# Moving the elementwise work off POOL in a two-layer hybrid attention and mixture-of-experts encoder

## The chip, the cores and the metric

The kernel runs on 1 core of a Trainium2 chip. The metric is device microseconds of one execution; the median of three runs of the kernel before is 1399.47 us (1397.34 to 1400.84). The engines are named as in the profile: PE (matmul), PEld (its weight loads), DVE (vector), ACT (scalar), POOL (GpSimd), SP (sync, which here only issues DMAs).

## The reference

Two layers over x of 512 tokens by 1024 channels, all in float32, with a conditioning vector c. Each layer does:

```
mod = silu(c) @ w_ada[l] + b_ada[l];  sh1, sc1, g1, sh2, sc2, g2 = split(mod, 6)
h   = layer_norm(x) * (1 + sc1) + sh1
mix = mixer(h)
x   = layer_norm(ALPHA * x + g1 * mix, ln1_g, ln1_b)
h   = layer_norm(x) * (1 + sc2) + sh2
ffn = moe(h)
x   = layer_norm(ALPHA * x + g2 * ffn, ln2_g, ln2_b)
```

The mixer projects h once (w_in), runs a global grouped-query attention (branch A, 8 heads) and a dilated windowed attention (branch B, three groups of 4 heads, joined by their softmax denominators), then computes (g_a * (out_a @ w_pa) + g_b * (out_b @ w_pb)) @ w_o with sigmoid gates. The mixture of experts scores 16 experts, picks the best group of four and the two best experts in it, and adds their SwiGLU outputs (256 hidden channels each) with normalised weights.

## The kernel before

The 512 tokens are 4 tiles of 128 (`NT`). A product that must hold float32 accuracy is split: each operand is rounded to a high part (ACT, `ACT.copy` to float32r), the low part is the difference (DVE, `tensor_sub`), and three matmuls are summed (`gemm3`, L220). Weights are split the same way in `wsplit` (L195; cast L215, subtraction L216, 520 of each at 128x512). The order of instructions on each engine follows the program's order and the framework's own ordering by readiness; `tc.issue_after` (an instruction isn't issued before another) adjusts it in ten places. Every engine works through its queue in order, and a DMA is issued by the engine whose queue it is written on: SP (`SY`), ACT or POOL (`PO`).

The stages of a layer, with the names and lines that the change touches:

- **Head.** `head_first` (L349, layer 0) norms x, transposes it, applies scale and shift per channel (`apply`, L374) and makes the high part (ACT, L377) and the low part (L378), the odd k on POOL. `head_next` (L390) does the same for layer 1, tile by tile; the low part (L413) of group j = 3 (`HLP`) is on POOL.
- **Projections, attention.** `first_q`, `fill_b`, `fill_g`, `rope`, branch A and branch B. POOL takes a power for the RMS norm (`pool_rsqrt`, L283), zeroes two key tiles per layer, and in layer 0 writes zeros to the expert output y2 by DMA.
- **Join and merge.** `join` (L886) weights branch B's three groups and adds them: the first addition on POOL (L892), the second on DVE (L893). The merge loop (L908 to L919) multiplies branch B's product by its gate (L915), adds branch A (L916; odd c, `PBPO`, on POOL), and splits the sum (ACT L918, DVE L919).
- **Output projection, norms.** For tile t and block b of 256 columns `out_block` (L941) multiplies the product by g1 (DVE, L947) and adds it to the residual xr (L948, POOL but for the two blocks in `XDVE`). `tile_x1` transposes xr for the router (PE), takes statistics and norms xr to x1; `tile_h2` norms x1 to h2, which a DMA on SP's queue stores to `h2d` in DRAM (L978). `norm` (L313): the first `cut` columns on DVE in two `scalar_tensor_tensor` steps (L321, L323), the rest on ACT (L319, scale and bias) and POOL (L325 times g, L326 plus b). `cut` is 768 for x1 and for xo, 896 for h2, 1024 for x1 of tile 3.
- **Router.** The last h2 is finished behind the sigmoid: ACT scales it (L1006), POOL adds the shift (L1007), in halves, and SP stores it (L1008). Expert weights ahead of use are loaded on SP's queue from L997 on. DVE compares scores in the tile `versus`, cleared by POOL (L1026), and with PE builds the index tile `vt` (L1076). POOL clears three tiles `xe` (L1100), then gathers the rows of expert e from `h2d` by an indirect DMA (`x_load`, L1106).
- **Expert loop.** For 16 experts: `x_split`, `x_gate`, `x_up` (the product with SiLU, L1138), `x_down` (products L1175, scaled by g2 L1176, scattered to y2 by an indirect DMA on POOL, L1180; the last two experts' outputs are kept in SBUF).
- **Combine.** y2 comes back in 8 tiles on SP's queue (L1296). `rows_in` adds them to x1 with their weights: `scalar_tensor_tensor` on DVE (L1306), except (t, 0) of every tile t (`PROWS`), where ACT scales (L1303) and POOL adds (L1304). The rows of tile 0 are added ahead of `x_down` of the last expert, those of tile 1 behind its first mark, those of tiles 2 and 3 behind its third (`SPLIT`). `combine` (L1332) adds the kept experts and x1 on PE in PSUM (L1312, L1335); `finish` (L1339) norms to xo and stores it, and in layer 0 goes on to layer 1's head.

`stats` (L300) issues on DVE the statistics (L303, L305) and var + eps (L285), then on POOL the power (L286) and minus mean times it (`nb`, L308).

Of the kernel before, what the change touches and what calls it, by code (L numbers as in the profile page):

```python
# [8 lines left out]
F32 = mybir.dt.float32  # L9
# [3 lines left out]
AF = mybir.ActivationFunctionType  # L13
# [12 lines left out]
NG = 4  # L26
# [61 lines left out]
def build(tc, A, out):  # L88
    nc = tc.nc
    with ExitStack() as es:  # L90
# [222 lines left out]
        def norm(src, name, g, b, st=None, cut=None):  # L313

            cut = cut or CUT
            m, r, nb = st or stats(src)
            n = f4(name, [D])
            for p, z in parts(src, cut, D) if cut < D else []:
                issued["act"] = ACT.activation(n[:, z], p, AF.Identity, bias=nb, scale=r)  # L319
            for p, z in parts(src, 0, cut):  # L320
                V.scalar_tensor_tensor(n[:, z], p, m, g[:, z], op0=OP.subtract, op1=OP.mult)  # L321
            a, z = slice(0, cut), slice(cut, D)
            issued["dve"] = V.scalar_tensor_tensor(n[:, a], n[:, a], r, b[:, a], op0=OP.mult, op1=OP.add)  # L323
            if cut < D:
                PO.tensor_tensor(n[:, z], n[:, z], g[:, z], op=OP.mult)  # L325
                PO.tensor_tensor(n[:, z], n[:, z], b[:, z], op=OP.add)  # L326
            return n
# [21 lines left out]
        def head_first(xt):  # L349
# [24 lines left out]
            def apply(k):  # L374
                z, H, L = (u[k // 2][:, k % 2, :] for u in (zT, hH, hL))
                i = V.tensor_scalar(z, z, mcol[0, 1][:, k:k + 1], mcol[0, 0][:, k:k + 1], op0=OP.mult, op1=OP.add)
                ACT.copy(H, z)  # L377
                (PO if k % 2 else V).tensor_tensor(L, z, H.bitcast(F32), op=OP.subtract)  # L378
                return i
# [10 lines left out]
        def head_next(l):  # L390
# [4 lines left out]
            def tile_in(t, x, st):  # L395
# [3 lines left out]
                for q in range(2):  # L399
# [10 lines left out]
                    for j in range(2 * q, 2 * q + 2):  # L410
                        f, H, L = F[:, 2 * j:2 * j + 2, :], hH[j][:, :, tcols(t)], hL[j][:, :, tcols(t)]
                        ACT.copy(H, f)  # L412
                        i = (PO if j in HLP else V).tensor_tensor(L, f, H.bitcast(F32), op=OP.subtract)  # L413
                        if j not in HLP:
                            issued["head"] = i
# [14 lines left out]
        def layer(l, hH, hL, W0, after=None, qk=None):  # L430
# [455 lines left out]
            def join():  # L886
                for i in range(2):
# [4 lines left out]
                    PO.tensor_tensor(oB[0][:, i, :], oB[0][:, i, :], oB[1][:, i, :], op=OP.add)  # L892
# [15 lines left out]
            for b in range(2):  # L908
                WB = wsplit(wb[:, 512 * b:512 * b + 512].rearrange("(k p) n -> p k n", p=P), [2, 512])
                for c in range(4):  # L910
# [5 lines left out]
                    (PO if c in PBPO else V).tensor_tensor(ga, ga, gb, op=OP.add)  # L916
# [22 lines left out]
            x1, r1, LAST = [], [], []  # L939

            def out_block(t, b):  # L941
# [6 lines left out]
                (V if (t, b) in XDVE else PO).tensor_tensor(xr[t][:, cb], xr[t][:, cb], y, op=OP.add)  # L948

            def tile_x1(t):  # L950
# [9 lines left out]
                n = norm(xr[t], "x1", r_g, r_b, st, D if t == NT - 1 else None)  # L960
# [4 lines left out]
            def tile_h2(t):  # L965
                n = x1[t]
                st = stats(n)
                V.scalar_tensor_tensor(sco[:, t], lg[:, t], r1[t], brow, op0=OP.mult, op1=OP.add)
                V.scalar_tensor_tensor(sco[:, t], sco[:, t], st[1], rrow, op0=OP.mult, op1=OP.add)
                if t < NT - 1:  # L970
                    n2 = norm(n, "h2", r_sc2, r_sh2, st, CUTH)
                    ACT.mul(n, n, ALPHA)
                else:
                    n2 = f4("h2", [D])
                    V.scalar_tensor_tensor(n2, n, st[0], r_sc2, op0=OP.subtract, op1=OP.mult)
                    LAST.append((n2, st[1]))
                    return
                SY.dma_start(h2d[tcols(t), :], n2)  # L978
# [21 lines left out]

            sig = ACT.activation(sco, sco, AF.Sigmoid)
            with tc.issue_after(sig.ins):
                n2, r = LAST[0]
                for i in range(2):
                    z = slice(512 * i, 512 * i + 512)
                    ACT.mul(n2[:, z], n2[:, z], r)  # L1006
                    PO.tensor_tensor(n2[:, z], n2[:, z], r_sh2[:, z], op=OP.add)  # L1007
                SY.dma_start(h2d[tcols(NT - 1), :], n2)  # L1008
                ACT.mul(x1[NT - 1], x1[NT - 1], ALPHA)
            sel = rt("sel", [NT, NE])  # L1010
# [14 lines left out]
            versus = sc("versus", [(NT + 1) * NG, 16])  # L1025
            PO.memset(versus, 0.0)  # L1026
# [70 lines left out]

            xes = [f4("xe", [D]) for _ in range(NXE)]
            for z in xes:
                PO.memset(z, 0.0)  # L1100
# [198 lines left out]
            def rows_in(n):  # L1299
                for _ in range(2 * n):  # L1300
                    t, k, y = ys.pop(0)
                    if (t, k) in PROWS[l]:
                        ACT.mul(y, y, gt[:, k, t:t + 1])  # L1303
                        PO.tensor_tensor(x1[t], x1[t], y, op=OP.add)  # L1304
                    else:
                        V.scalar_tensor_tensor(x1[t], y, gt[:, k, t:t + 1], x1[t], op0=OP.mult, op1=OP.add)  # L1306
# [32 lines left out]
            def finish(t):  # L1339
                y, st = Y.pop(t)  # L1340
                n = norm(y, "xo", r_g, r_b, st, CUT2[l])
# [22 lines left out]
HLP = (3,)  # L1364
XDVE = ((3, 2), (3, 3))
# [8 lines left out]
PROWS = (((0, 0), (1, 0), (2, 0), (3, 0)),) * 2  # L1374
EKEEP = 2
CUTH = 896
PBPO = (1, 3)
# [7 lines left out]
CUT = 768  # L1385
NPE = 3
CUT2 = (768, 768)
# [25 lines left out]
```

## Time and profile before

| | before |
|---|---|
| median of 3 runs | 1399.47 us |
| the profiled execution's own time | 1398.57 us |
| its span, first to last instruction | 1396.8 us |
| PE busy | 1278.9 us (92%) |
| PEld busy | 1039.7 us (74%) |
| DVE busy | 1024.2 us (73%) |
| ACT busy | 720.2 us (52%) |
| POOL busy | 282.4 us (20%) |
| mean granted PE clock | 0.967 of full speed |
| DMA | 266.76 MB, mean 191 GB/s |

Times in the profile are microseconds from the span's start unless marked ns. A row of a timeline is a start, a duration, the engine, the line of the kernel, the operation, output <- inputs, the count and, in brackets, how long the engine stood idle before it and what ended that. Queues of the engines that only issue carry a q (ACTq, SPq).

### The profile page before, as it was taken

What the parts mean: (1) busy time and instruction counts of PE and PEld (TensorE: products, weight loads), DVE (VectorE), ACT (ScalarE), POOL (GpSimd) and SP (SyncE); (2) the same over time, 40 slices, a digit from 0 to 9 for tenths busy, and PEclk for the clock granted to TensorE, in tenths of its full rate; (3) what the DMA queues carried; (4) which work ended last, traced back from release to release, by engine and by line L of the source; (5) the groups of instructions that cost most, each with busy time, mean ns of one, the idle gap of its engine ahead of it and who ended that gap; (6) DMA issues with size and microseconds to landing.
All of it is one profiled execution on the core that took longest, in us unless ns stands there. A gap on an engine that the chain in (4) does not pass through costs nothing. (4 is left out here: it accounts for less than half of the span.)

```text
span 1396.8 us, 21644 instructions
## 1 busy us (share of the span) xinstructions
PE 1278.9 (92%) x7953; PEld 1039.7 (74%) x7953; DVE 1024.2 (73%) x1974; ACT 720.2 (52%) x1506; POOL 282.4 (20%) x273
## 2 busy tenths in 40 slices
PE   5898999999998949999889999999999894999986
PEld 4797777677777938888659787767777784888862
DVE  5877777767367778999798877564336767899985
ACT  2344444555644237777645444455565522777760
POOL 1132000000002651221341300000000256222224
PEclk9999999999999969999999999999999996999998
DMA  9646654556155187999653555122214536799952
GB/s 317 218 156 239 208 167 167 154 185 218 32 174 204 61 272 260 308 346 338 233 182 125 160 181 170 61 76 76 76 46 151 180 122 218 272 301 344 352 206 84
DMA packets 182992, 266.76 MB, mean 191 GB/s; under 512 B 18665, under 2 KB 131721, under 8 KB 182880
## 3 DMA queue, kind: packets, MB, share of 16 engines
q1 hardware_dynamic: 159312, 225.46, 48.4%
q0 software_dynamic: 11456, 24.07, 4.9%
q10 hardware_dynamic: 12112, 15.78, 3.7%
q8 instruction: 64, 1.05, 0.3%
q14 instruction: 48, 0.39, 0.1%
HBM read 250.79 MB, written 27.30 MB: 199 GB/s over the span
## 5 line engine op out<-in xcount | busy, mean ns | idle before, releaser
L216 DVE TENSOR_TENSOR wL<-raw,wH 128x512 fp32r<-128x512 f32 x520 | 349.9, 703 | 67.3 <-ACT wH L215 52.0
L215 ACT CAST wH<-raw 128x512 fp32r<-128x512 f32 x520 | 318.9, 622 | 148.4 <-PE mm L1175 41.6
L225 PE MATMUL mm<-hH,wH 128*128 128x512 f32 x512 | 206.4, 403 | 0.0
L226 PE MATMUL mm<-hL,wH 128*128 128x512 f32 x512 | 202.4, 395 | 0.0
L227 PE MATMUL mm<-hH,wL 128*128 128x512 f32 x512 | 202.0, 394 | 0.0
L225 PE MATMUL mm<-wH,xH 128*128 128x256 f32 x512 | 149.1, 291 | 1.0 <-ACT xH L343 1.0
L227 PE MATMUL mm<-wH,xL 128*128 128x256 f32 x512 | 148.9, 291 | 0.9 <-DVE xL L344 0.9
L226 PE MATMUL mm<-wL,xH 128*128 128x256 f32 x512 | 146.6, 286 | 0.3 <-DVE wL L216 0.3
L249 DVE SCALAR_TENSOR_TENSOR acc<-araw,cond,acc 128x512 f32<-128x512 f32 x148 | 110.7, 749 | 5.5 <-DMA araw<-in_w_ada 2.3
L227 PEld LDWEIGHTS mm<-hH,wL 128*128 128x128 f32 x512 | 96.2, 188 | 21.1 <-issue 1.1
L225 PEld LDWEIGHTS mm<-hH,wH 128*128 128x128 f32 x512 | 96.3, 188 | 20.1 <-issue 1.2
L226 PEld LDWEIGHTS mm<-hL,wH 128*128 128x128 f32 x512 | 96.3, 188 | 19.1 <-issue 0.3
L225 PEld LDWEIGHTS mm<-wH,xH 128*128 128x128 f32 x512 | 99.0, 193 | 3.1 <-ACT xH L343 2.0
L226 PEld LDWEIGHTS mm<-wL,xH 128*128 128x128 f32 x512 | 98.9, 193 | 2.4 <-DVE wL L216 1.2
L227 PEld LDWEIGHTS mm<-wH,xL 128*128 128x128 f32 x512 | 98.6, 192 | 2.3 <-DVE xL L344 1.8
L225 PE MATMUL mm<-wH,hH 128*128 128x256 f32 (+1 forms) x272 | 81.7, 301 | 4.6 <-ACT hH L412 2.8
L227 PE MATMUL mm<-wH,hL 128*128 128x256 f32 (+1 forms) x272 | 81.2, 300 | 2.1 <-DVE hL L378 0.7
L226 PE MATMUL mm<-wL,hH 128*128 128x256 f32 (+1 forms) x272 | 80.5, 296 | 0.1
L1180 POOL DMA_INDIRECT y<-ye,vt x28 | 33.6, 1202 | 209.8 <-DVE ye L1176 209.8
L281 POOL DMA_DIRECT2D mod<-adar x8 | 4.3, 532 | 331.4 <-ACT adar L280 331.4
L1175 PE MATMUL mm<-raw,eT 128*128 128x512 f32 x128 | 65.4, 635 | 3.6 <-ACT eT L1158 1.5
L745 DVE TENSOR_TENSOR zB<-sB,biasB 128x256 f32<-128x256 f32 (+2 forms) x48 | 22.8, 488 | 61.4 <-PE sB L743 27.7
(316 smaller groups left out, 2873.0 us busy)
## 6 DMA issues: line engine op xcount, KB each, us to landing
araw<-in_w_ada SPq DMA_DIRECT2D x44, 1024.0 KB, 5.3
raw<-in_w_in SPq DMA_DIRECT2D x40, 1024.0 KB, 5.2
raw<-in_w_exp_gate SPq DMA_DIRECT2D x32, 1024.0 KB, 9.3
raw<-in_w_exp_up SPq DMA_DIRECT2D x28, 1024.0 KB, 12.4
raw<-in_w_exp_down SPq DMA_DIRECT2D x28, 1024.0 KB, 10.0
raw<-in_w_out SPq DMA_DIRECT2D x8, 1024.0 KB, 7.2
y<-y SPq DMA_DIRECT2D x16, 512.0 KB, 8.4
eraw<-in_w_ada SPq DMA_DIRECT2D x4, 1024.0 KB, 16.0
```

The source lines that it names most:

```text
L215: ACT.copy(H, raw(s))
L216: V.tensor_sub(L, raw(s), H.bitcast(F32))
L225: PE.matmul(o, lhsT=lH, rhs=rH, start=(i == 0), stop=False)
L226: PE.matmul(o, lhsT=lH, rhs=rL, start=False, stop=False)
L227: PE.matmul(o, lhsT=lL, rhs=rH, start=False, stop=(i == n - 1))
L249: last = V.scalar_tensor_tensor(acc, raw[:, k, :], ck, acc, op0=OP.mult, op1=OP.add)
L281: PO.dma_start(moddr[l, kind].rearrange("o (k n) -> (o k) n", n=P), r[0:8, :])
L745: V.tensor_add(z, s[:, :, 0:wid], biasB[g][:, ii::2, j0:j0 + wid])
L1175: PE.matmul(p, lhsT=a, rhs=w, start=(i == 0), stop=(i == len(todo) - 1))
L1180: st = PO.indirect_dma_start(out=y2, out_offset=bass.IndirectOffsetOnAxis(ap=vidx[:, e:e + 1], axis=0), in_=ye, in_offset=None, bounds_che ...
```

## The change

All elementwise instructions of POOL but the small ones of `stats` and of the RMS norm, and the zeroing of key tiles, go to DVE; the clearing of `versus` and of the xe tiles goes to ACT, which multiplies a row by zero. `norm` no longer divides a tile between engines: two steps on DVE for columns 0 to 255 and 256 to 1023 (three where the source is two PSUM tiles), then one step over all 1024. The last h2 is normed like the others and stored at once on ACT's queue. The constants `HLP`, `XDVE`, `PROWS`, `CUTH`, `PBPO`, `CUT` and `CUT2` go. In the diff a line of "..." marks what is left out.

```diff
-        def norm(src, name, g, b, st=None, cut=None):
-
-            cut = cut or CUT
+        def norm(src, name, g, b, st=None):
+
             m, r, nb = st or stats(src)
             n = f4(name, [D])
-            for p, z in parts(src, cut, D) if cut < D else []:
-                issued["act"] = ACT.activation(n[:, z], p, AF.Identity, bias=nb, scale=r)
-            for p, z in parts(src, 0, cut):
-                V.scalar_tensor_tensor(n[:, z], p, m, g[:, z], op0=OP.subtract, op1=OP.mult)
-            a, z = slice(0, cut), slice(cut, D)
-            issued["dve"] = V.scalar_tensor_tensor(n[:, a], n[:, a], r, b[:, a], op0=OP.mult, op1=OP.add)
-            if cut < D:
-                PO.tensor_tensor(n[:, z], n[:, z], g[:, z], op=OP.mult)
-                PO.tensor_tensor(n[:, z], n[:, z], b[:, z], op=OP.add)
+            for lo, hi in ((0, 256), (256, D)):
+                for p, z in parts(src, lo, hi):
+                    V.scalar_tensor_tensor(n[:, z], p, m, g[:, z], op0=OP.subtract, op1=OP.mult)
+            V.scalar_tensor_tensor(n, n, r, b, op0=OP.mult, op1=OP.add)
             return n
...
-                (PO if k % 2 else V).tensor_tensor(L, z, H.bitcast(F32), op=OP.subtract)
+                V.tensor_sub(L, z, H.bitcast(F32))
...
-                        i = (PO if j in HLP else V).tensor_tensor(L, f, H.bitcast(F32), op=OP.subtract)
-                        if j not in HLP:
-                            issued["head"] = i
+                        issued["head"] = V.tensor_sub(L, f, H.bitcast(F32))
...
-                    PO.tensor_tensor(oB[0][:, i, :], oB[0][:, i, :], oB[1][:, i, :], op=OP.add)
+                    V.tensor_add(oB[0][:, i, :], oB[0][:, i, :], oB[1][:, i, :])
...
-                    (PO if c in PBPO else V).tensor_tensor(ga, ga, gb, op=OP.add)
+                    V.tensor_add(ga, ga, gb)
...
-                (V if (t, b) in XDVE else PO).tensor_tensor(xr[t][:, cb], xr[t][:, cb], y, op=OP.add)
+                V.tensor_add(xr[t][:, cb], xr[t][:, cb], y)
...
+                n2 = norm(n, "h2", r_sc2, r_sh2, st)
+                (SY if t < NT - 1 else ACT).dma_start(h2d[tcols(t), :], n2)
                 if t < NT - 1:
-                    n2 = norm(n, "h2", r_sc2, r_sh2, st, CUTH)
                     ACT.mul(n, n, ALPHA)
-                else:
-                    n2 = f4("h2", [D])
-                    V.scalar_tensor_tensor(n2, n, st[0], r_sc2, op0=OP.subtract, op1=OP.mult)
-                    LAST.append((n2, st[1]))
-                    return
-                SY.dma_start(h2d[tcols(t), :], n2)
...
+            versus = sc("versus", [(NT + 1) * NG, 16])
+            ACT.mul(versus.rearrange("p a b -> p (a b)"), r_sc2[:, 0:(NT + 1) * NG * 16], 0.0)
             sig = ACT.activation(sco, sco, AF.Sigmoid)
+            xes = [f4("xe", [D]) for _ in range(NXE)]
             with tc.issue_after(sig.ins):
-                n2, r = LAST[0]
-                for i in range(2):
-                    z = slice(512 * i, 512 * i + 512)
-                    ACT.mul(n2[:, z], n2[:, z], r)
-                    PO.tensor_tensor(n2[:, z], n2[:, z], r_sh2[:, z], op=OP.add)
-                SY.dma_start(h2d[tcols(NT - 1), :], n2)
                 ACT.mul(x1[NT - 1], x1[NT - 1], ALPHA)
+                for z in xes:
+                    ACT.mul(z, r_sc2, 0.0)
...
-            versus = sc("versus", [(NT + 1) * NG, 16])
-            PO.memset(versus, 0.0)
...
-            xes = [f4("xe", [D]) for _ in range(NXE)]
-            for z in xes:
-                PO.memset(z, 0.0)
...
-                    if (t, k) in PROWS[l]:
-                        ACT.mul(y, y, gt[:, k, t:t + 1])
-                        PO.tensor_tensor(x1[t], x1[t], y, op=OP.add)
-                    else:
-                        V.scalar_tensor_tensor(x1[t], y, gt[:, k, t:t + 1], x1[t], op0=OP.mult, op1=OP.add)
+                    V.scalar_tensor_tensor(x1[t], y, gt[:, k, t:t + 1], x1[t], op0=OP.mult, op1=OP.add)
...
-                n = norm(y, "xo", r_g, r_b, st, CUT2[l])
+                n = norm(y, "xo", r_g, r_b, st)
```

## Rows read from the trace of the kernel before

**Rows 1.** Busy time by stretch: merge (layer 0), output projection (layer 0), between the layers.
```profile
core 0: us, PE busy (x) PEld busy (x) DVE busy (x) ACT busy (x) POOL busy (x), PEclk, DMA share, GB/s
418.45:437.70 19.25, 15.39 (x85) 12.64 (x84) 17.61 (x26) 9.51 (x15) 5.98 (x4) 1.00 0.32 106
440.00:494.70 54.70, 52.17 (x417) 50.62 (x418) 37.33 (x69) 16.30 (x23) 30.80 (x40) 0.97 0.44 150
...
692.00:740.00 48.00, 42.38 (x175) 26.64 (x174) 39.00 (x82) 25.25 (x55) 22.53 (x29) 0.91 0.52 180
```

**Rows 2.** PE's waits in the whole span: for whom, us in total, times, longest.
```profile
PE pos L1049 <- DVE rt_o L1044: 23.1, 2, 11.7
...
PE tp L336 <- DVE ea L1138: 8.9, 2, 5.1
```

**Rows 3.** DVE's groups, shapes apart: count | busy us, mean ns | idle before.
```profile
L919 DVE TENSOR_TENSOR mL<-gate,mH 128x512 fp32r<-128x512 f32 x16 | 16.3, 1020 | 3.2 <-ACT mH L918 2.5
...
L915 DVE TENSOR_TENSOR gate<-pb,gate 128x512 f32<-128x512 f32 x16 | 10.6, 683 | 0.0
...
L323 DVE SCALAR_TENSOR_TENSOR x<-x,rstd,row 128x1024 f32<-128x1024 f32 x2 | 2.6, 1286 | 0.9 <-POOL rstd L286 0.9
```

**Rows 4.** Timelines of DVE and POOL, head of layer 0.
```profile
48.55 1.76 DVE L378 TENSOR_TENSOR hL<-zT,hH 128x512 fp32r<-128x512 f32 x1
...
55.11 1.35 POOL L378 TENSOR_TENSOR hL<-zT,hH 128x512 fp32r<-128x512 f32 x1 [1.01 <-ACT hH L377]
```

**Rows 5.** Timelines of DVE, POOL and SP, router of layer 0.
```profile
501.92 1.15 DVE L1022 TENSOR_TENSOR versus<-rt_sel 128x48 f32<-128x48 f32 x1
502.96 1.27 DVE L1021 TENSOR_TENSOR versus<-rt_gs 128x12 f32<-128x12 f32 x1
...
505.88 1.03 DVE L1041 TENSOR_SCALAR asgb<-rt_rank 128x64 bf16<-128x64 f32 x1
...
510.02 0.19 DVE L1076 TENSOR_TENSOR vt<-c_none,mp 128x32 int32<-128x32 f32 x1 [0.25 <-PE mp L1071]
...
501.70 2.49 POOL L1007 TENSOR_TENSOR h<-h,row 128x512 f32<-128x512 f32 x2 [0.85 <-ACT h L1006]
504.13 2.73 POOL L1100 MEMSET xe<- 128x1024 f32 x3
512.59 1.19 POOL L1106 DMA_INDIRECT xe<-h2d,vt  x1 [5.73 <-DVE rt_we L1197]
...
504.22 0.34 SPq L1008 DMA_DIRECT2D h2d<-h  x1
```

**Rows 6.** Timelines of POOL, DVE and PE, last expert of layer 0.
```profile
684.30 2.38 POOL L1304 TENSOR_TENSOR x<-x,y 128x1024 f32<-128x1024 f32 x1 [9.14 <-ACT y L1303]
...
684.76 2.47 DVE L216 TENSOR_TENSOR wL<-raw,wH 128x512 fp32r<-128x512 f32 x1 [2.64 <-ACT wH L215]
...
691.09 0.41 DVE L1138 TENSOR_TENSOR ea<-ea,mm 128x256 f32<-128x256 f32 x1
...
679.40 1.98 PE L1175 MATMUL mm<-raw,eT 128*128 128x512 f32 x4 [0.52 <-ACT eT L1158]
...
691.55 0.69 PE L336 MATMUL tp<-c_ident,ea 128*128 128x128 f32 x2 [5.06 <-DVE ea L1138]
...
693.75 3.43 PE L1175 MATMUL mm<-raw,eT 128*128 128x512 f32 x4
```

**Rows 7.** Timeline of ACT and its queue: the last xr load of layer 0, its first use.
```profile
438.19 0.33 ACTq L928 DMA_DIRECT2D xr<-in_x  x1
...
446.34 1.06 ACT L929 ACTIVATE xr<-xr 128x1024 f32<-128x1024 f32 x1 [0.69 <-DMA xr<-in_x]
```

**Rows 8.** Timelines of DVE and POOL, router of layer 1.
```profile
1179.93 0.19 DVE L1076 TENSOR_TENSOR vt<-c_none,mp 128x32 int32<-128x32 f32 x1 [0.25 <-PE mp L1071]
...
1180.94 1.18 POOL L1106 DMA_INDIRECT xe<-h2d,vt  x1 [4.17 <-DVE rt_den L1086]
```

**Rows 9.** Timelines of DVE and POOL, the last tile of layer 1.
```profile
1384.76 0.21 DVE L305 BATCH_NORM_AGGREGATE mv<-st 128x2 f32<-128x12 f32 x1
...
1387.63 1.34 POOL L326 TENSOR_TENSOR xo<-xo,row 128x256 f32<-128x256 f32 x1
```

More of the change, by code (lines that the diff above doesn't have):

```diff
@@ L938, in layer @@
             h2d = dr.tile([S, D], F32, name=f"h2d{l}")
-            x1, r1, LAST = [], [], []
+            x1, r1 = [], []
             def out_block(t, b):
@@ L959, in tile_x1 @@
                 r1.append(st[1])
-                n = norm(xr[t], "x1", r_g, r_b, st, D if t == NT - 1 else None)
+                n = norm(xr[t], "x1", r_g, r_b, st)
                 x1.append(n)
@@ L1363 @@
 FDV = (0, 1, 4)
-HLP = (3,)
-XDVE = ((3, 2), (3, 3))
 BEHIND = ((0, "gate"), (0, "up"))
@@ L1373 @@
 SPLIT = ((1, 1, 0, 2), (1, 1, 0, 2))
-PROWS = (((0, 0), (1, 0), (2, 0), (3, 0)),) * 2
 EKEEP = 2
-CUTH = 896
-PBPO = (1, 3)
 OPAT = (1, 3)
@@ L1384 @@
 AHEAD = 2
-CUT = 768
 NPE = 3
-CUT2 = (768, 768)
 ADA = ((4, 5, 8, 9, 6, 7, 10, 11, 14, 15, 12, 13, 16, 17), (8, 9, 6, 7, 10, 11))
```

## The prediction

> **How I read it.** I began with busy time by stretch. PE is busy 92% of the span (the table above), so a change to the elementwise engines can pay only where PE isn't full. In the merge of the gated branches PE is busy 15.39 of 19.25 us while DVE is busy 17.61: DVE paces it. In the output projection PE has 52.17 of 54.70 us: PE paces it, and DVE has 17 us to spare. Between the layers both are loaded, DVE with 39.00 of 48 us [rows 1]. PE's waits, read next, show where else PE stands: 23.1 us in two waits for the router, and 8.9 us in two waits for the SiLU product of the last expert [rows 2].
>
> Then I compared each DVE form with itself at a place where POOL is quiet. L915 and L919 are both two-input 128x512 instructions: 683 ns against a mean of 1020 [rows 3]. The timelines say why: a DVE instruction that starts during a POOL one stays until that one is over. L378 takes 1.76 us beside POOL's own L378 [rows 4]. A 48-element comparison takes 1.15 and a 12-element one 1.27 while POOL adds L1007 [rows 5]. A subtraction L216 starts 0.46 us after POOL's row add of 2.38 and takes 2.47, so that it ends 0.55 after it [rows 6]. POOL's work is not free: where the two meet, it costs DVE as much as doing it would.
>
> **Prices.** A 512-wide two-input DVE instruction is 0.68 us and a 1024-wide one 1.29, so 512 more columns cost 0.60, also back to back; 256-wide is then an estimated 0.38 [rows 3].
>
> **What DVE gains in work.** Sixteen at 512 (four L378, four L892, eight L916): 10.9 us. Thirty-two at 256 (28 L948, four L413): 12.2. Ten at 1024 (eight row adds, two last steps of h2): 12.9. Norms: 512 more columns over the two steps of six x1 and eight xo, 256 more in six h2: 8.4 + 1.8. Together 46.2 us, on an engine idle for some 370. What counts is the place.
>
> **Head of layer 0.** Four low parts leave POOL, whose last runs from 55.11 to 56.46. Three DVE instructions there are lengthened by about 1.0 each, of which one is shown (1.76 for 0.68) [rows 4]. DVE loses 3.1 and gains 4 x 0.60, and the last part takes 0.68 instead of 1.35: first products -1.4, and -0.2 for the hop between engines: -1.6 (bounds -0.5, if ACT's casts set the pace, and -3).
>
> **Join and merge.** L892 lies under branch A's product, with PE full: I cost it at nothing; without that cover it would be four times 0.68. In the merge, per layer, DVE loses (1.020-0.683) x 8 = 2.7 of lengthening and an estimated 1.1 of waiting for POOL's first add by way of ACT's cast, and gains four L916, 2.4: -1.4, for both layers -2.8 (bounds 0 and -5).
>
> **Output projection.** DVE gains 14 x 0.38 + 3 x 0.60 + 3 x 0.30 = 8.0 us per layer, under the 17 to spare. PE's transposes get the residual sooner, by one hop and a shorter add. But L948 of a tile whose xr comes late (446.34 for the last [rows 7]) now holds DVE's queue, and behind it the weight splits and the products mix that PE's PSUM tiles wait for. I take -0.5 per layer, -1.0 (bounds +3 and -3).
>
> **Router.** PE has nothing to do from the last tile to the first gathered rows, so here DVE's chain counts fully. Gone: 1.15 + 1.27 less 0.2 each (the 32-element L1076 takes 0.19), and about 0.7 of the 1.03 of L1041, which runs under POOL's clearing [rows 5]: 2.7. Added: the last 1024-wide step of h2, 1.29, part of which fills the wait for ACT's sigmoid: +1.0. DVE should meet the last tile some 0.6 earlier, since x1's last columns no longer come back from POOL. So the index tile vt is ready 2.3 earlier. The clearing of three tiles goes to ACT behind the sigmoid, some 3 us on an engine that is idle there; it costs nothing as long as it ends before the gather.
>
> The first gather doesn't follow vt at once: 510.21 to 512.59 in layer 0, 1180.12 to 1180.94 in layer 1 [rows 5, 8]. I read the gap as the wait for the last store of h2d, issued at 504.22 behind megabytes of weights on SP's queue. After, it is issued near 502 on ACT's. At best it lands before vt: the gather is 2.3 + 2.2 = 4.5 earlier in layer 0, 2.3 + 0.7 = 3.0 in layer 1. At worst it takes what an xr load on ACT's queue took beside SP's weights, from 438.19 to 446.34, 8.2 us [rows 7], and lands near 510.2: 2.3 and 0.8 earlier. No row is nearer to either end, so the middles, -3.4 and -1.9: -5.3 (bounds -2 and -7.5).
>
> **Between the layers.** Before, ACT scaled y rows ahead of the last expert's weight casts, DVE's two subtractions stood behind two POOL adds, and the product L1138 came at 691.09. PE had waited 5.06 for it and came back slow: four passes of L1175 take 3.43 at 693.75, 1.98 at 679.40 [rows 6]. Gone are 1.79 for each of the two subtractions (one is shown) and ACT's scaling, an estimated 1; one more row add stands in front, 1.25: -3.3 at least and 5.06 at most, I take -4.3. The clock that isn't lost gives 1.45 for those passes and as much for the ones around them: -2.9. Against it, in a stretch where DVE is the bound, stand the row adds of the last two tiles (2.6), four norms (2.4) and four low parts (1.5), less an estimated 2 of its 9 idle us that go: +4.5. Sum -2.7 (bounds +1 and -5).
>
> **Last combine.** The same start: PE's second wait is 8.9-5.06 = 3.8 [rows 2, 6]; of it -2.8, and -1.2 of clock. Then PE's product with the identity paces the tiles. The tail from the last statistics on went DVE, POOL, ACT, POOL: 1384.76 to 1388.97, 4.2 us [rows 9]. On DVE it is 0.5 for the first small steps, 1.3 for three pieces, 1.29: -1.1. Sum -5.1 (bounds -2 and -6.5).
>
> **Total.** 1.6 + 2.8 + 1.0 + 5.3 + 2.7 + 5.1 = 18.5 less. The profiled execution took 1398.57, 0.9 under the median of 1399.47; from the median that makes 1381. The far ends all at once would be 1369 and 1399. A measurement of this kernel can tell about 0.3%, 4 us, from no change.
>
> **Rivals.** *DVE becomes the bound*, and the kernel slower. The place is the output projection and the stretch between the layers: what it takes over there (2 x 8.0, and 9.1 with all four row adds) would lie on the path, 25.1, and the other terms give back 14.8: +10.3, 1410. It decides once DVE's queue collects 9 us of waits in a projection (54.70 less 37.33 and 8.0), and between the layers if 9.1 more don't fit in 9.0 idle us, where it is close. Against it: much of that idle time is waiting for POOL.
>
> *ACT's queue gives the store nothing.* The xr load shows the queues sharing [rows 7]; and if the store is queued ahead of the sigmoid, ACT holds that until h2 is done. Then the router gives 2.0 instead of 5.3: 1384. The Trainium skill's page DMA: Bandwidth & Descriptors, section Issuing engines are not separate DMA queues, says that starting transfers from several engines saves only the issuing time. By that rule the store would land earlier by its earlier issue alone; no row before has a store on ACT's queue.
>
> *The expert weights set the pace.* If their stream limits the expert loops, what the router wins, 5.3, is lost again: 1386. Against it: in both waits that end a loop PE waits for a product, not for a load.
>
> *The lengthening is not POOL's doing.* Then DVE only gains work, mostly hidden: 1399. The matching ends speak against it [rows 4 to 6]. Nor does POOL go idle: it keeps the powers L286, L308 and the descriptors, and DVE's two-input steps can still hold up a power.
>
> **Chances.** Forecast (1372 to 1389) 0.62; store 0.13; weights 0.11; no gain 0.06; DVE bound 0.08. Faster 0.86, same 0.06, slower 0.08. The range takes in the first three with their bounds: 1370 to 1392.
>
> **What would show it.** L919 near 0.69; L1021 and L1022 near 0.2; no L216 over 0.8 in the last expert; each wait of PE for that product under 1 us; the gather within 0.3 us of vt; the head's last low part by 55; 3 us from the last statistics to the last store. I am wrong if PE's wait for the router stays above 22, if PE waits longer for xr, or if the stretch between the layers grows.

## The result and the profile after

The changed kernel takes 1384.88 us (median of 5 runs, 1382.22 to 1386.66) against 1397.96 for the kernel before (median of 5 runs): ratio 0.9894, 95% interval 0.9875 to 0.9912. That is faster by 1.1%; the two medians alone differ by 13 us, 0.9%. The time is inside the range (1370 to 1392) and 4 us above the 1381 predicted. The sum of the terms was 18.5; the two profiled spans differ by 1396.8 - 1383.1 = 13.7.

The first part of the page says that the work moved as it was meant to: POOL has 165 instructions left, and DVE is busy 75% of the span. Summed by instruction, DVE's groups that took over work grew by 45.8 us (46.2 in the prediction) and its other groups lost 27.3, of which 8.9 in the 520 subtractions L216; its busy time, in which overlapping ends count once, grew by 12.6 only.

```profile
span 1383.1 us, 21523 instructions
PE 1273.1 (92%) x7953; PEld 1034.4 (75%) x7953; DVE 1036.8 (75%) x2056; ACT 704.8 (51%) x1482; POOL 165.0 (12%) x165
```

PE's waits are the best single view of what the change did (for whom; us in total, times, longest):

```profile
PE pos L1033 <- DVE asgb L1025: 18.7, 2, 9.3
PE tp L330 <- DMA xe<-h2d,vt: 14.8, 2, 8.9
...
PE tp L330 <- ACT x L326: 9.1, 1, 9.1
...
PE y L1288 <- DVE rstd L285: 4.9, 1, 4.9
```

The wait for the router's ranks fell from 23.1 to 18.7 and the 8.9 us for the last expert's product are gone [rows 2]. Three waits grew: for the first gathered rows (12.9 before, 14.8 now), for ACT's first normalization (4.3 before) and, new, for the statistics between the layers. DVE's groups, shapes apart, show that the lengthening is gone (count | busy us, mean ns | idle before); the one at 1020 ns in [rows 3] is now 681:

```profile
L907 DVE TENSOR_TENSOR gate<-pb,gate 128x512 f32<-128x512 f32 x16 | 10.8, 683 | 0.0
L911 DVE TENSOR_TENSOR mL<-gate,mH 128x512 fp32r<-128x512 f32 x16 | 10.6, 681 | 0.0
L320 DVE SCALAR_TENSOR_TENSOR x<-x,rstd,row 128x1024 f32<-128x1024 f32 x8 | 10.2, 1276 | 0.0
```

To hold each term against the trace I cut both spans at the same marks: first branch product pb, first and last projection product mo, first gathered tile on PE, first product with the identity (L1311), fourth copy of q and k, the last product with the identity (each product by its start), the end. The last column is a second profile of the changed kernel (experiment changed_again).

| us, after less before | predicted | changed | again |
|---|---|---|---|
| head and attention, layer 0 | -1.6 | -0.3 | -1.1 |
| merge, both layers | -2.8 | -3.1 | -3.2 |
| output projection, both | -1.0 | -4.5 | -4.8 |
| router, both | -5.3 | +0.5 | -0.2 |
| experts of layer 0, with the last one's wait and clock | -7.2 | -7.5 | -6.7 |
| first product with the identity to the fourth copy | +4.5 | +11.2 | +10.4 |
| attention, layer 1 (not touched) | 0 | -1.8 | +0.8 |
| experts of layer 1, with the same wait | -4.0 | -5.8 | -4.6 |
| after the last product with the identity | -1.1 | -2.5 | -2.5 |
| sum | -18.5 | -13.7 | -11.8 |

Two terms failed most, the router and the stretch between the layers; the experiments are about these first.

### The profile page after: what moved, and what is told of

Its sections match the earlier page's. It is cut to its first block, busy times and chain, and to the rows that moved or that the text cites. A ratio compares the mean times of both kernels' runs of the same rounds, so it can differ in the third digit from the quotient of the medians.

```text
span 1383.1 us, 21523 instructions
## 1 busy us (share of the span) xinstructions
PE 1273.1 (92%) x7953; PEld 1034.4 (75%) x7953; DVE 1036.8 (75%) x2056; ACT 704.8 (51%) x1482; POOL 165.0 (12%) x165
## 5 line engine op out<-in xcount | busy, mean ns | idle before, releaser
L216 DVE TENSOR_TENSOR wL<-raw,wH 128x512 fp32r<-128x512 f32 x520 | 340.3, 686 | 58.2 <-ACT wH L215 43.7
L286 POOL TENSOR_TENSOR rstd<-rstd,c_mhalf 128x1 f32<-128x1 f32 x32 | 20.4, 638 | 438.4 <-DVE rstd L285 438.4
L225 PEld LDWEIGHTS mm<-wH,hH 128*128 128x128 f32 (+1 forms) x272 | 53.6, 197 | 7.2 <-ACT hH L406 4.0
```

The costliest lines, as they stand in the source:

```text
L216: V.tensor_sub(L, raw(s), H.bitcast(F32))
L225: PE.matmul(o, lhsT=lH, rhs=rH, start=(i == 0), stop=False)
L286: PO.tensor_tensor(r, r, mhalf[:, :n], op=OP.pow)
```

## Experiments between the layers

The stretch from the first product with the identity to the fourth copy, as the windows show it (us; then busy us of PE, PEld, DVE, ACT, POOL with instructions, granted clock, DMA share, GB/s), before and after:

```profile
698.39:742.59 44.20, 38.58 (x182) 25.87 (x181) 38.68 (x85) 22.83 (x52) 18.97 (x29) 0.96 0.41 144
```
```profile
687.58:742.96 55.38, 42.94 (x182) 29.32 (x181) 43.18 (x97) 23.05 (x52) 7.90 (x16) 0.85 0.42 149
```

DVE is busy for 4.5 us more, but the stretch grew by 11.2. The predicted +4.5 was something else: 6.5 us of added work, less 2 us of idle time that the work was to fill. DVE's idle time did not fall, it rose from 5.5 to 12.2 us, and this 6.7 is the whole miss. The same 182 instructions on PE took 42.94 us at a granted clock of 0.85 against 38.58 at 0.96: PE waited, and came back slower. The start of the stretch on DVE before, and on DVE, ACT and PE in the changed kernel:

```profile
701.59 1.29 DVE L303 BATCH_NORM_STATS2 st<-y 128x6 f32<-128x512 f32 x2
702.79 2.48 DVE L216 TENSOR_TENSOR wL<-raw,wH 128x512 fp32r<-128x512 f32 x4
```
```profile
688.55 4.86 DVE L1282 SCALAR_TENSOR_TENSOR x<-y,rt_gt,x 128x1024 f32<-128x1024 f32 x4
695.33 2.50 DVE L216 TENSOR_TENSOR wL<-raw,wH 128x512 fp32r<-128x512 f32 x4 [1.92 <-ACT wH L215]
697.75 1.88 DVE L303 BATCH_NORM_STATS2 st<-y 128x6 f32<-128x512 f32 x3
...
694.68 2.18 ACT L215 CAST wH<-raw 128x512 fp32r<-128x512 f32 x4 [10.22 <-DMA raw<-in_w_in]
...
701.26 3.78 PE L1288 MATMUL y<-yk,G 128*128 128x512 f32 x4 [4.93 <-DVE rstd L285]
```

With all row adds on DVE, the order in which its instructions are issued came out differently: the four splits of the next layer's first weights stand ahead of the first tile's statistics (before, behind L303; in rows_on_pool below, with half of the row adds back on POOL, behind it again). Those weights land near 694.7, so DVE idles 1.92 us and splits for 2.5 while the statistics, which DVE could have run from 693.4 on, wait, and behind them PE.

**split_behind_stats** puts the splits behind:

```
-            W0 = w_block(l + 1, 0) if nxt else None
+            W0 = None
+            raw0 = wraw(A["w_in"][l + 1][:, 0:256].rearrange("(k p) n -> p k n", p=P), [8, 256]) if nxt else None
...
                 combine(i)
+                if nxt and i == 0:
+                    W0 = wsplit(raw0, [8, 256], behind=[issued["aggr"]])
```

> The changed kernel with one edit in the order: the four splits of the next layer's first weight block stand on DVE behind the statistics of the first combined tile, not ahead of them. Theory (in the changed kernel DVE stood before that split for weights that had not landed: 1.92 us of idling, then 2.50 of work, while the statistics were ready near 693.4 and ran at 697.75): the statistics start near 693.5, PE's wait for the third tile's PSUM (4.93 us) falls under 1.5, the stretch between the layers ends 3 to 5 us earlier, and the time is 3 to 5 us less, about 1381. Rival (DVE's amount of work bounds the stretch, the order only moves it about): within 1 us of 1384.9.

```profile
693.82 1.28 DVE L303 BATCH_NORM_STATS2 st<-y 128x6 f32<-128x512 f32 x2
695.14 0.21 DVE L305 BATCH_NORM_AGGREGATE mv<-st 128x2 f32<-128x12 f32 x1
695.27 0.65 DVE L216 TENSOR_TENSOR wL<-raw,wH 128x512 fp32r<-128x512 f32 x1
```

The statistics run at 693.82, the stretch takes 52.54 us (688.08 to 740.62), 2.8 less. PE's wait fell only to 3.1, not under 1.5. The time, 1382.8, is 2 us lower, but its ratio 0.9894 (0.9874 to 0.9913) can't be told from the changed kernel's. So the order is worth 2.8 of the 6.7 us by which the term was missed, as these two profiles have it. Seven profiles that keep the changed kernel's order here have 53.61 to 56.33 us, 54.7 in the mean, so 2.8 may be anything from 1 to 4.

**rows_on_pool** takes four of the eight row adds back to ACT and POOL:

```
+                    if k == 0:
+                        ACT.mul(y, y, gt[:, k, t:t + 1])
+                        PO.tensor_tensor(x1[t], x1[t], y, op=OP.add)
+                    else:
+                        V.scalar_tensor_tensor(x1[t], y, gt[:, k, t:t + 1], x1[t], op0=OP.mult, op1=OP.add)
```

> The changed kernel with four of the eight row adds of each layer back on ACT (scaling) and POOL (add). Theory (POOL's adds hold DVE up in the last expert): subtractions L216 over 1.5 us come back in the last expert, PE waits 4 to 5 us for the product L1118 in layer 0 and 2 to 4 in layer 1, the gain at the end of layer 0's expert loop goes (6 to 7 us later there), but the stretch between the layers, which gave that gain back in the changed kernel, takes some of it up again; layer 1's end is 4 to 5 later. Time 4 to 8 us more than 1384.9. Rival (the lengthening is not POOL's doing): within 1 us, no L216 over 0.8 us.

POOL and DVE in the last expert of layer 0, and PE's wait over the span:

```profile
683.40 2.34 POOL L1284 TENSOR_TENSOR x<-x,y 128x1024 f32<-128x1024 f32 x1 [0.86 <-ACT y L1283]
...
683.61 2.68 DVE L216 TENSOR_TENSOR wL<-raw,wH 128x512 fp32r<-128x512 f32 x1
...
PE tp L330 <- DVE ea L1118: 7.9, 2, 4.1
```

The subtraction that started 0.21 us after POOL's add took 2.68 instead of 0.69 and ended 0.55 after it, as in [rows 6]; PE waits 7.9 us again. The first product with the identity comes at 693.67, 6.1 later than in the changed kernel. The time is 1388.25, ratio 0.9934 (0.9919 to 0.9949): more by 5.6 us as the ratios have it and by 3.4 as the medians do, where the theory said 4 to 8. But the stretch after it takes only 47.76 us, and the fourth copy comes at 741.43 instead of 742.96 (741.50 in changed_again). In layer 0, then, moving the row adds to DVE gains nothing: what the last expert wins, the stretch behind it loses. The gain is layer 1's, where no next layer stands behind: there the experts take 179.00 us instead of 173.58 (174.79 in changed_again).

**last_rows_behind**, on top of the three edits described below, moves the last tile's two row adds of each layer behind the first statistics:

```
+                if i == 0:
+                    with tc.issue_after(issued["aggr"].ins):
+                        rows_in(1)
...
-SPLIT = ((1, 1, 0, 2), (1, 1, 0, 2))
+SPLIT = ((1, 1, 0, 1), (1, 1, 0, 1))
```

> The three edits and a fourth: the two row adds of the last tile stand on DVE behind the statistics of the first combined tile and the small step after them, not ahead of them. Theory (of the stretch between the layers, DVE's queue order is what is lost: the first tile was ready near 691.0 and its statistics ran at 693.17 with the three edits): they start 2 us earlier, PE's wait for the third tile's PSUM falls from 3.1 to about 1, each layer's end comes 1 to 2 us earlier, and the time is 2 to 3 less than with the three edits, about 1377.5. Rival (the amount of work on DVE bounds the stretch; the adds only move): within 1 us of 1380.1.

The rival's number holds. The statistics start at 689.42, but the second tile's only at 697.21: the weights' split stands between, and DVE waits 1.27 us for it. PE's wait, which was to fall to 1, rose from 3.1 to 4.7. So this shows that the new order gains nothing, not that the amount of work is the bound. The stretch takes 52.50, with the three edits 52.58; the time is 1379.56 (ratio 0.9849, 0.9824 to 0.9874) against 1380.08 (0.9859).

**three_edits_xo_shared** gives xo's norm its three engines back (ACT and POOL have 256 of the 1024 columns):

```
+            if name == "xo":
...
+                for p, z in parts(src, 768, D):
+                    ACT.activation(n[:, z], p, AF.Identity, bias=nb, scale=r)
...
+                PO.tensor_tensor(n[:, z], n[:, z], g[:, z], op=OP.mult)
+                PO.tensor_tensor(n[:, z], n[:, z], b[:, z], op=OP.add)
```

> The three edits, with the norm of the tiles between the layers and at the end (xo) shared over three engines as before the change: ACT normalizes the last 256 columns, POOL scales and adds, DVE does 768. Theory A (what is lost between the layers is DVE's added work): 0.6 us of DVE less for each tile, the stretch between the layers 2 to 4 us shorter, the time 1 to 3 less than with the three edits. Theory B (POOL's two steps hold up DVE and come back with a longer way from engine to engine): the stretch no shorter, the last norm some 1 us longer at the end, the time 1 to 2 more.

Windows of the stretch and of the end (here from the last tile's first product with the identity on, 1.29 us ahead of its last):

```profile
685.41:733.39 47.98, 39.73 (x182) 26.53 (x181) 40.83 (x93) 24.89 (x57) 14.86 (x24) 0.93 0.49 170
1360.50:1377.90 17.40, 3.59 (x9) 1.33 (x7) 6.74 (x13) 1.13 (x2) 5.74 (x8) 0.67 0.22 90
```

Each theory holds in one place. Between the layers 2.4 us less of DVE's work, and 2.2 us less of its idle time, shorten the stretch by 4.6 against the three edits. At the end the shared norm costs 3.5 us (17.40 against 13.94): 1.6 up to the last step's end, 1.8 behind it (the last section shows why). The time is 1379.28 (ratio 0.9847), which can't be told from the three edits' 1380.08.

**shared_between_only** takes each where it pays:

```
-                n = norm(y, "xo", r_g, r_b, st)
+                n = norm(y, "xo", r_g, r_b, st, bool(nxt))
```

> The three edits, with xo's norm shared over ACT, POOL and DVE between the layers only, and on DVE alone in the last combine. Theory (two places, two answers: between the layers DVE's work is the bound, and the shared norm shortened that stretch by some 4.6 us; at the end the way from engine to engine is, and DVE alone ended 3.5 us sooner after the last product with the identity): both are had, the stretch between the layers takes some 48 us from the first product with the identity to the last of the four q and k copies, the end comes 14 us after the last such product, and the time is 3 to 5 less than with the three edits, 1375 to 1377. Rival (the two results were noise, or the order of the work shifts again): 1379 or more.

```profile
span 1370.7 us, 21530 instructions
681.91:729.64 47.73, 39.34 (x182) 26.51 (x181) 40.84 (x93) 24.90 (x57) 14.83 (x24) 0.93 0.49 174
```

It takes 1374.02 us (1372.54 to 1376.13), ratio 0.9817 (0.9803 to 0.9832): 26 us less than the kernel before, 11 less than the changed one, and 1 less than expected. Of the 11.2 us, by single profiles, the order was 2.8 (55.38 to 52.54) and the norms 4.8 (52.54 to 47.73). The 3.5 left are 2.2 of DVE's work and 1.4 of its idle time against the kernel before; what of them is row adds and what low parts (2.6 and 1.5 in the prediction) was not tried.

## Experiments on the router

After the change, ACT's queue issues the store at 499.13, vt is written at 504.93, and the gather goes at 509.21:

```profile
499.62 0.24 DVE L1008 TENSOR_TENSOR versus<-rt_sel 128x48 f32<-128x48 f32 x1
499.74 0.18 DVE L1007 TENSOR_TENSOR versus<-rt_gs 128x12 f32<-128x12 f32 x1
...
504.93 0.19 DVE L1060 TENSOR_TENSOR vt<-c_none,mp 128x32 int32<-128x32 f32 x1 [0.25 <-PE mp L1055]
...
499.13 0.35 ACTq L963 DMA_DIRECT2D h2d<-h  x1
...
509.21 1.35 POOL L1086 DMA_INDIRECT xe<-h2d,vt  x1 [11.40 <-DVE wL L216]
```

The comparisons take 0.24 and 0.18 instead of 1.15 and 1.27 [rows 5]. But from vt to the gather it is 4.3 us, before 2.6: the gather waits longer for the store. From its issue to the gather there are 10.1 us; before, on SP's queue, 8.4.

**store_on_sp_last** moves only the queue: the store is on SP's, behind the same loads.

```
+            with tc.issue_after(lastw.ins):
+                SY.dma_start(h2d[tcols(NT - 1), :], issued["h2"])
```

> The changed kernel with the store of the last h2 tile on SP's queue, this time behind the last loads of expert weights, so that the same bytes stand ahead of it as with ACT's queue and only the queue differs. Theory (what is on its way sets the landing, and ACT's queue gives nothing): 8 to 10 us from issue to landing, the gather some 4 us after vt in layer 0 and 1 to 2 in layer 1, time within 1.5 us of the changed kernel. Rival (a queue of its own gives the store a share of the transfers at once): it lands 3 us or more later than on ACT's queue in layer 0, and the time is 3 to 6 us more.

**store_on_sp** is the plain way back to SP; there SP issues the store ahead of its last two loads of expert weights, 1 MB.

```
-                (SY if t < NT - 1 else ACT).dma_start(h2d[tcols(t), :], n2)
+                SY.dma_start(h2d[tcols(t), :], n2)
```

> The changed kernel with the store of the last h2 tile on SP's queue as before the change; there it stands ahead of the last two half-megabyte loads of expert weights, which SP now issues after it. Theory (the store's landing is set by the bytes that are on their way when it is issued, not by the queue): 1 MB less is ahead of it, at some 390 GB/s 2.7 us, so the store lands near 505 in layer 0 instead of 507.8, the gather follows vt by 1.5 us instead of 4.1, in layer 1 by some 0.5 instead of 1.3, and the time is 2 to 4 us less. Rival (ACT's queue of its own gives the store a way past the weights): the store takes 3 us or more longer than the 8.7 from issue to landing, the gather comes later, and the time grows by 3 to 6 us.

The two, SP's queue and POOL's gather, first store_on_sp_last, then store_on_sp with its vt:

```profile
493.31 2.53 SPq L191 DMA_DIRECT2D raw<-in_w_exp_down  x2
498.00 0.34 SPq L992 DMA_DIRECT2D h2d<-h  x1
...
508.14 1.31 POOL L1093 DMA_INDIRECT xe<-h2d,vt  x1 [12.29 <-DVE wL L218]
```
```profile
498.17 0.36 SPq L963 DMA_DIRECT2D h2d<-h  x1
498.57 1.53 SPq L189 DMA_DIRECT2D raw<-in_w_exp_down  x2
...
503.98 0.19 DVE L1060 TENSOR_TENSOR vt<-c_none,mp 128x32 int32<-128x32 f32 x1 [0.25 <-PE mp L1055]
...
505.43 1.17 POOL L1086 DMA_INDIRECT xe<-h2d,vt  x1 [9.43 <-DVE rt_gt L1073]
```

Behind the same bytes, SP's queue takes 10.1 us from issue to gather, just what ACT's takes; with the last loads behind it, 7.3, and the gather follows vt by 1.5 us. In layer 0 the store's place among the bytes decides, the queue nothing. So says the Trainium skill, DMA: Bandwidth & Descriptors, Issuing engines are not separate DMA queues: transfers run on the same DMA engines whichever engine starts them; the rows agree. Layer 0's gain stays to the end of its experts (last product L1118 at 679.57 instead of 682.74), which speaks against the rival that the expert weights set the pace. In layer 1 the gather follows vt by 1.0 instead of 1.5 us, and the profile shows no gain there. The times: store_on_sp_last 1387.08, ratio 0.9907 (0.9884 to 0.9930), store_on_sp 1382.49, 0.9887 (0.9872 to 0.9901). The first is at the edge of what was expected of no change; neither can be told from the changed kernel by its time.

## Experiments on the other terms

**merge_on_pool** and **residual_on_pool** each put one kind of add back on POOL:

```
-                    V.tensor_add(ga, ga, gb)
+                    (PO if c in (1, 3) else V).tensor_tensor(ga, ga, gb, op=OP.add)
```
```
-                V.tensor_add(xr[t][:, cb], xr[t][:, cb], y)
+                (V if (t, b) in ((3, 2), (3, 3)) else PO).tensor_tensor(xr[t][:, cb], xr[t][:, cb], y, op=OP.add)
```

> The changed kernel with the merge's adds of every second column block back on POOL. Theory (POOL's 128x512 adds lengthen the DVE instructions beside them, and the merge is paced by DVE): L907's and L911's mean rises from some 0.7 to about 1 us, each merge takes 1.2 to 1.7 us longer, and the time grows by 2.5 to 3.5. Rival (PE paces the merge): less than 0.5 us for each merge.

```profile
L911 DVE TENSOR_TENSOR mL<-gate,mH 128x512 fp32r<-128x512 f32 x16 | 18.0, 1128 | 1.1 <-ACT mH L910 0.6
L907 DVE TENSOR_TENSOR gate<-pb,gate 128x512 f32<-128x512 f32 x16 | 10.7, 682 | 0.0
```

Each merge takes 1.6 us longer (14.03 and 13.75 against 12.46 and 12.19), the time is 1388.14, ratio 0.9917 (0.9893 to 0.9940), 3 more, with an interval that overlaps the changed kernel's: the theory, but for L907, which stays at 682. Its first input is in PSUM, while L911 reads both from SBUF. The Trainium skill, SBUF — State Buffer, Who interferes with whom, says that DVE's instructions with two SBUF inputs contend with POOL's reads, and that those with at most one don't, outside two-port modes, which a tensor_tensor doesn't have; these two rows agree.

> The changed kernel with the residual adds of the output projection (L940) back on POOL, all but the last tile's last two. Theory (the projection gained 2.6 us in layer 0 and 1.9 in layer 1 because PE's transposes at a tile's end no longer wait for a POOL add and the hop to it): both projections take 1.5 to 2.5 us longer and the time grows by 3 to 5. Rival (PE paces the projection, and the gain there came from elsewhere, for instance from x1 and h2 whose last columns no longer come from POOL): under 1 us for both.

Neither theory: the projections take 1.0 and 0.3 us longer (59.03 and 59.26 against 58.06 and 58.93), less than half of the 2.6 and 1.9 gained. The time, 1386.43, ratio 0.9917 (0.9904 to 0.9930), is more by 1.6 as the medians have it and by 3 as the ratios do, with overlapping intervals; the projections explain 1.3.

Where the rest of the gain comes from was not tried, but the kept traces narrow it down. The projection of layer 0 before, in the changed kernel and here:

```profile
430.54:491.15 60.61, 57.25 (x457) 55.53 (x455) 43.24 (x74) 18.90 (x27) 30.64 (x37) 0.97 0.43 145
```
```profile
428.80:486.86 58.06, 55.83 (x456) 54.35 (x456) 47.90 (x95) 15.28 (x21) 9.42 (x12) 1.00 0.44 151
```
```profile
431.04:490.07 59.03, 55.74 (x456) 54.15 (x456) 44.62 (x82) 16.19 (x21) 21.48 (x26) 1.00 0.43 148
```

In layer 0 the rest is PE's clock: 57.25 us of PE work at 0.97 before, 55.74 at 1.00 here; why it was lower before isn't shown. In layer 1 the clock is 1.00 in all three, and PE's waits for the residual, in the same order, are these:

```profile
PE tp L336 <- POOL xr L948: 3.1, 3, 1.3
```
```profile
PE tp L330 <- DVE xr L940: 0.8, 2, 0.5
```
```profile
PE tp L330 <- POOL xr L940: 1.7, 3, 0.8
```

Of the 2.3 us of waiting that went, the add itself accounts for 0.9. What took the other 1.4 stays open; the norms' columns that left POOL are what remains of the change there.

**changed_again** is the changed kernel once more.

> The changed kernel once more, to see how much its stages move from run to run, and beside the kernels of this group. Theory (the later start of the first normalization on ACT, 17.3 to 19.0 us in the profiles of the changed kernel and its variants against 12.74 before, belongs to the program): it starts at 17 to 19 again, PE's wait for it is 8.5 to 10 us, the time is within 2 us of 1384.9. Rival (chance): it starts near 13 and PE waits 4 to 5.

1384.68 us, ratio 0.9896 (0.9877 to 0.9915). ACT's first normalization starts at 17.22, PE waits 8.7 for it: the late start belongs to the program. ACT stands in the issue of a small column load, which took 2.51 us before:

```profile
10.68 7.02 ACTq L854 DMA_DIRECT2D gb<-in_ln_b  x1
17.80 3.50 ACT L326 ACTIVATE x<-x,nb,rstd 128x1024 f32<-128x1024 f32 x3 [13.19 <-DMA gb<-in_ln_g]
```

**columns_behind_head** issues these loads later:

```
+                    order.enter_context(tc.issue_after(issued["plain"].ins))
+                for i, n in enumerate(("ln1_g", "ln1_b")):
...
```

> The changed kernel with the two column loads of ln1's scale and offset (layer 0) issued on ACT's queue behind the four first normalizations, not ahead of them. Theory (the issue of the second one, 7.02 us, holds ACT): the first normalization starts near 13 instead of 17.8, PE's wait for it is 4 to 5 us instead of 9.1, DVE's first modulation comes near 42 instead of 43.6, where the landing of the modulation weights sets it, and the time is 1 to 3 us less. Rival (the router's weight load, issued before them, holds ACT just as long, or the modulation weights set the head's pace in any case): the first modulation moves by less than 0.5 us and the time by less than 1.

```profile
PE tp L330 <- ACT x L326: 4.4, 1, 4.4
...
39.66 3.11 DVE L249 SCALAR_TENSOR_TENSOR acc<-eraw,cond,acc 128x512 f32<-128x512 f32 x4 [2.46 <-DMA eraw<-in_w_ada]
...
43.08 0.55 DVE L370 TENSOR_SCALAR zT<-zT,mc,mc 128x512 f32<-128x512 f32 x1
```

PE's wait halves, and nothing follows: DVE's first modulation comes at 43.08 (43.16 in changed_again), since the modulation weights land no sooner. 1384.44, ratio 0.9894 (0.9872 to 0.9916). The rival holds.

**three_edits** joins split_behind_stats, store_on_sp and columns_behind_head.

> Three edits on the changed kernel together: the split of the next layer's first weights behind the first statistics, the last h2 store on SP's queue ahead of the last loads, the column loads behind the first normalizations. Theory (they act in three places and add up): some 2.5, 2.5 and 1.5 us less, together about 6, 1378 to 1380. Rival (what one gains, a later wait takes back, as between the layers): 1382 or more.

1380.08 us (1374.70 to 1384.00), ratio 0.9859 (0.9835 to 0.9882), about 5 us less than changed_again beside it (0.9896, 0.9877 to 0.9915). The two intervals touch, and none of the three edits could be told from no change by its own time; the third is worth nothing by its profile either.

## Why the prediction was right, and where its steps failed

**Direction** was right, and so was the cause: POOL's work held up DVE. In rows_on_pool the long subtractions come back with POOL's adds, in merge_on_pool L911's 1128 ns. The rival that the lengthening is not POOL's doing falls.

**The size** was right in part by luck. Of the prediction's six terms only the merge and the head lie within their bounds (the head with the attention behind it in the second profile alone). The router and the stretch between the layers gave less than their bounds allow: taken whole, with the last expert of layer 0, the latter was to give -2.7 (+1 at worst) and gave +3.7 in both profiles. The output projection and the last combine gave more: -4.5 and -8.3, where -3 and -6.5 were the best. All the rows of the table together, the untouched attention of layer 1 among them, gave 13.8 us too little and 9.1 too much, which leaves the 5 by which the sum is off.

**The signs** that the prediction named were met by L911 (681 ns), the comparisons (0.24 and 0.18), the subtractions of the last expert (none above 0.8), PE's wait for the product there (gone) and the last combine (3.2 us). Two were not: the gather came 4.3 us after vt, and the head's last low part ended at 56.96. Of the three signs of being wrong one came true: the stretch between the layers grew, which the prediction's own sum let it do by 4.5 and no more.

**Merge** (-2.8, measured -3.1) and the **start of the last combine** (-4.3 and -2.9 in layer 0, measured -7.5 together; -4.0 in layer 1, measured -4.6 to -5.8) were sized from the right rows.

**Router** (-5.3, measured about 0). Three steps failed. "DVE should meet the last tile some 0.6 earlier": from the last projection product to the sigmoid it took 10.0 us in layer 0, 9.4 in changed_again, 9.6 before. DVE's chain from the sigmoid to vt lost 1.2 us (9.27 to 8.06), not 1.7; the difference is that most of h2's first step now stands between the sigmoid and the comparisons (0.81 us from the sigmoid's start to the router's next instruction on DVE instead of 0.29). And the store: "the middles" between two far bounds was the wrong choice. It kept behind the bytes on their way, and the gap to the gather grew by 1.7 and 0.5 us. That is the rival "ACT's queue gives the store nothing"; its price of 1384 is what was measured, but by coincidence, since other terms moved too.

**Between the layers** (+4.5, measured +11.2). The step that failed is "less an estimated 2 of its 9 idle us": DVE was to fill idle time with the added work, and it idled 6.7 us more (12.2 instead of 5.5), since the issue order changed, the chain from tile to tile got longer by more than the added work, and PE's clock fell from 0.96 to 0.85. The rival "DVE becomes the bound" named the place; its price was for two other stretches too, one of which, the projection, went the other way.

**Output projection** (-1.0, measured -4.5) was mis-sized: in layer 0 PE ran the same instructions at a granted clock of 1.00 instead of 0.97 (55.83 us of PE work against 57.25), which the prediction left out, and in layer 1 it waited 0.8 us for the residual instead of 3.1.

**Head** (-1.6, measured -0.3 and -1.1 with the attention behind it): DVE's part, from the first modulation to the last low part, did get shorter, from 14.45 us (42.01 to 56.46 on POOL) to 13.38 (43.58 to 56.96), but it began 1.6 later (1.2 in changed_again). Why stays open: columns_behind_head brought ACT's normalization forward and not this start.

**Tail** (-1.1, measured -2.5): the part named, from the last statistics to the last step, took 3.2 us instead of 4.2; a further 1.8 came from behind it, and 0.4 went ahead of it. The path was wrong: the end follows POOL's last instruction, not the last step (last section).

## What to carry to other kernels

In this kernel, work taken from the helper engine paid where it had held up a chain that others wait for, and not everywhere: between the layers the norm was 4.6 us faster on three engines, at the end 3.5 us faster on one. When work moves, read the new issue order of the engine that takes it: an instruction that waits for a late load may now stand ahead of one that everybody waits for. To make a store land sooner, look at the bytes issued ahead of it, not at its queue. And see which engine's last instruction the end of the program waits for: here it was POOL's.

## What was not expected

The end of the span. From the end of the last elementwise step it took 7.8 us before (1388.97 to 1396.8) and 7.8 in three_edits_xo_shared (1370.09 to 1377.9), where POOL has the last step; 6.0 in the changed kernel (1377.10 to 1383.1) and 5.9 in shared_between_only (1364.77 to 1370.7), where DVE has it. Four kernels agree on some 1.8 us. No run was made for it, but the kept traces show what it is. POOL's queue ends the program with a closing step (DRAIN), and its next event comes 7.0 us after POOL's last instruction. Before and in the changed kernel (of the events the durations in ns, then the first and the last start in us):

```profile
1387.63 1.34 POOL L326 TENSOR_TENSOR xo<-xo,row 128x256 f32<-128x256 f32 x1
...
L1409 POOLq EVENT_SEMAPHORE  x4: 17/17/17, 1396.0 to 1396.7; - x4
```
```profile
1375.01 0.27 POOL L308 TENSOR_SCALAR nb<-mv,rstd 128x1 f32<-128x1 f32 x1
...
L1378 POOLq EVENT_SEMAPHORE  x4: 17/17/17, 1382.3 to 1383.0; - x4
```

The span ends 7.8 us after POOL's last instruction in every one of the fourteen profiles, whatever that instruction is. SP's queue, with the last store landed, is through earlier (1380.26 in the changed kernel). With the last step on DVE, POOL's last instruction is the small `nb`, 1.8 us ahead of that step's end. From the last product with the identity it comes after 7.3 us before and 4.9 in the changed kernel, which is the tail's whole 2.5.

The issue of the small column load on ACT's queue took 2.51 us before and 6.2 to 7.7 in every profile of the changed kernel and its variants that has it there, with the same loads issued in the same order. That stays open, and costs nothing here.
